# Whole-chunk 32-row products, grouped transposes, and no 32-row unit for the first expert

## The chip, the cores and the metric

One core of a Trainium2 chip runs the whole kernel. The metric is the device time of one execution in microseconds (us). The engines that matter here are TensorE (PE in the profile: matrix products; PEld is its loading of the stationary operand), VectorE (DVE), ScalarE (ACT), GpSimd (POOL, which issues gathers and scatters) and SyncE (SP, which issues the loads of weights).

## What is computed

A layer with token mixers and then a mixture of experts over 1024 tokens. The change lies in the expert stage and in the routing just ahead of it. Cut to that part, the reference is:

```
logits = h @ w_router + b_router
probs = softmax(logits).reshape(n_tok, 4, 4)
g_sel = argmax(top_k(probs, 2)[0].sum(-1), -1)
top_w, top_i = top_k(probs[token, g_sel], 2)
weight = top_w / sum(top_w)
expert = g_sel * 4 + top_i
...
y_blk = (silu(xb @ w_g[e]) * (xb @ w_u[e])) @ w_d[e]
...
y = sum(y_blk[dest] * weight, 1)
x = x + gt2 * y
return rms_norm(x, g_final)
```

There are 16 experts; each takes 1024 features to 1536 and back. Every token goes to two of them, 2048 slots in all. Everything is float32. With the inputs of the reference the sixteen experts receive 124, 123, 98, 103, 151, 157, 145, 139, 99, 152, 152, 85, 172, 80, 138 and 130 rows (worked out from the reference).

## The kernel before

**Pages.** An expert's weights come in 18 pages of 1 MB, each 128 x 2048: twelve for gate and up (`w_gu`), six for down (`w_d`). `load` takes the next page from `order` and issues it on SyncE into one of ten page buffers (tiles `praw` and `raw`); a buffer is free again when its last reader is done. `part` splits a page for products of full accuracy out of the faster float32r format: ScalarE rounds the page to its high part, VectorE subtracts to get the low part, and both stand in a tile `hl` with three buffers (lines 1186 and 1187). `page` hands out the next split page.

**Rows of an expert.** The rows of an expert are laid out as a block of 128 (block A) and 0, 1 or 2 units of 32 rows more (block B). `UNITS` fixes the number for each place in the order of the experts: the first place is always the model's expert 0, the others are sorted by their number of rows at run time. Before, the first place has one unit, the second two, eight others one, and six none. Rows beyond 128 plus 32 for each unit go to a slow loop at the end of the kernel (`overflow_block`), which is skipped when there are none.

**Block A** (`block_a`, line 1366). Per page there are two slices of 128 features, and for each slice the three products high x high, high x low and low x high, each over two halves of 512 columns: twelve matmuls, accumulated in `pa`.

**Block B** (`block_b`, line 1378). The 32 rows of a unit are multiplied with the unsplit page in plain float32. The array is used as four column strips of 32: strip g holds the unit's rows and computes the columns 256 g to 256 g + 255. That is eight matmuls for a page and a unit; the trace has two records for each. With two units a product of zeros (`pb<-zz`, line 1372) opens the accumulation.

**The loop over experts.** Gate and up come in three chunks of four pages, then the six down pages. Before, the products go in pairs of pages: block B of two pages, block A of the same two pages, and so on. So a chunk has two blocks B and the down part three. After a chunk, ScalarE applies silu to the gate half and VectorE multiplies by the up half: `sa` from `pa`, `sb_` from `pb`. TensorE then turns them (transposes `aat`, `abt`, lines 1573 and 1578), and they are copied out: `aah` and `aal` by `split_a`, `abT` by ScalarE. They are the stationary operand of the down products. During the down pages `prep` turns the next expert's gathered rows (`xat`, `xbt`), and at the end the sums are scaled (`ya`, `yb`) and added to rows of `x1_d` by indirect DMAs of GpSimd (line 1422).

**The first expert.** `own_row` and `own_rows` find its rows before the table of all experts is ready: per block of 128 tokens a mark matrix `own` (line 1131), then small products (line 1139) and a few steps on VectorE that give `tk0` and `ch0`, whose values drive the first gathers (`first_xa`, `first_xb`). After its first chunk, `places` works out on VectorE the order of all other experts and their rows (lines 1311 to 1342); SyncE reads three words of it (`cnt`) before it can address the pages of the second expert.

**The order of instructions.** Each engine runs its own queue in order. A list scheduler orders the instructions; `tc.issue_after(x)` puts the instructions traced in its block behind x on x's engine. In the last expert (no unit), `tail` starts the final normalisation of the rows that are already complete.

Of the kernel before, what the change touches and what calls it, by code (L numbers as in the profile page):

```python
# [6 lines left out]
F32 = mybir.dt.float32  # L7
F32R = mybir.dt.float32r
BF16 = mybir.dt.bfloat16
# [44 lines left out]
UNITS = tuple(2 if r == 1 else 1 if r < 10 else 0 for r in RANK)  # L54
# [24 lines left out]
def constants():  # L79
    p = np.arange(128)  # L80
    s, t = p[:, None], p[None, :]
    f = np.concatenate([
        np.eye(128),
        np.ones((128, 128)),
        (s < t) * 1.0,
        (s % 32) == np.arange(2),
    ], 1).astype(np.float32)
    t64 = np.arange(64)[None, :]
    i = np.concatenate([
        (s % 64) <= t64, (s % 64) >= t64,  # L90
        2 * (s + 128 * (np.arange(16) // 2)[None, :]) + (np.arange(16) % 2)[None, :],
        np.broadcast_to(2 * (S + np.arange(CAP) % TRASH)[:, None], (CAP, 16)).reshape(128, 144),
    ], 1).astype(np.int32)
# [12 lines left out]
    sl[:, 3] = 15 - e + 65536 * (e == 0)  # L106
    c = np.arange(128)[None, :]
    g4, r = s // 32, s % 32
    trash = np.concatenate([S + s, 4 * (S + 128 + r) + g4, 4 * (S + 160 + r) + g4], 1)
    z = np.concatenate([  # L110
        np.broadcast_to(16 * np.concatenate([c, 128 + c % 32, 160 + c % 32], 1), (128, 384)),
        np.broadcast_to([[32, 128, 128]], (128, 3)), np.broadcast_to([[1, 4, 4]], (128, 3)),
        np.concatenate([0 * s, g4, g4], 1) - trash, trash,
        np.stack([s // 32 + 4 * np.arange(8)[None], np.broadcast_to(s % 32, (128, 8)), np.ones((128, 8)),
                  np.zeros((128, 8))], 2).reshape(128, 32),
    ], 1).astype(np.float32)
    return f, i, g.reshape(128, 96), ((s - t) % 32 == 0).astype(np.float32), z, sl.reshape(128, 64)
# [48 lines left out]
def body(tc, A, out):  # L166
# [778 lines left out]
    tk0, ch0 = (cp.tile([128, 3], I32, name=n) for n in ("tk0", "ch0"))  # L945
# [27 lines left out]
    kz = t1.tile([128, 428], F32, name="kz")  # L973
# [11 lines left out]
    V.tensor_copy(tri.rearrange("p i c -> p (i c)"), kz[:, 396:428])  # L985
# [142 lines left out]
    def own_row(i):  # L1128

        R = st_[i][5]  # L1130
        V.tensor_scalar(own[:, i, :], kz[:, 0:384], R[:, 7, 0:1], R[:, 5, 0:1], op0=ALU.is_equal, op1=ALU.mult)
        V.tensor_copy(tri[:, i, 3:4], R[:, 4, 0:1])

    def own_rows():

        p = ax("own")
        for b in range(3):
            for i in range(8):
                PE.matmul(p[:, 4 * b:4 * b + 4], own[:, i, 128 * b:128 * b + 128], tri[:, i, :], start=i == 0,
                          stop=i == 7)  # L1140
        f = t1.tile([128, 3, 4], F32, name="f3")
        V.tensor_copy(f.rearrange("p b c -> p (b c)"), p[:, 0:12])
        for c in range(3):
            V.tensor_mul(f[:, :, c], f[:, :, c], kz[:, 384 + 3 * c:387 + 3 * c])
        V.tensor_add(f[:, :, 0], f[:, :, 0], f[:, :, 1])
        V.tensor_add(f[:, :, 2], f[:, :, 2], kz[:, 393:396])
        V.tensor_add(f[:, :, 0], f[:, :, 0], f[:, :, 2])
        placed.append(V.tensor_copy(tk0, f[:, :, 0]))
        V.tensor_copy(ch0, f[:, :, 3])
# [10 lines left out]
    raws, ready = [], []  # L1160
# [17 lines left out]
    def load():  # L1178
        raws.append(page_tile([128, 2048]))
        e, n, i = order.pop(0)  # L1180
        return SP.dma_start(raws[-1], A[n][bass.ds(expert(e), 1), i].rearrange("o p n -> (o p) n") if e else A[n][0, i])

    def part():
        raw = raws.pop(0)
        hl = split_tile()
        SC.activation(hl[:, 0, :], raw, AF.Copy)  # L1186
        V.tensor_sub(hl[:, 1, :], raw, hl[:, 0, :].bitcast(F32))  # L1187
        ready.append(tuple(a.rearrange("p (k n) -> p k n", k=2) for a in (raw, hl[:, 0, :], hl[:, 1, :])))

    def page():  # L1190
        if not ready:
            if not raws:
                load()
            part()
        return ready.pop(0)
# [84 lines left out]
    with tc.issue_after(counted.ins), tc.issue_after(scaled.ins):  # L1280
        for i in range(2):
            part()
# [77 lines left out]
    def block_a(acc, st, k0, pg, start, stop):  # L1360

        _, wh, wl = pg
        for k in range(2):
            for n, (x, w) in enumerate(((0, wh), (0, wl), (1, wh))):
                for h in range(2):
                    PE.matmul(acc[h], st[x][:, k0 + k, :], w[:, k, 512 * h:512 * h + 512],  # L1366
                              start=start and (k, n) == (0, 0), stop=stop and (k, n) == (1, 2))

    def block_b(n, acc, st, k0, pgs, first, last):

        if n > 1 and first:
            PE.matmul(acc, zz[:, 0:128], zz, start=True, stop=False)
        for i, (w, _, _) in enumerate(pgs):
            for j in range(n):
                for k in range(2):
                    end = last and (i, j, k) == (len(pgs) - 1, n - 1, 1)
                    for g in range(4):
                        PE.matmul(acc[32 * g:32 * g + 32, 256 * j:256 * j + 256], st(j, k0 + 2 * i + k),
                                  w[:, k, 256 * g:256 * g + 256], start=n == 1 and first and (i, k) == (0, 0), stop=end,
                                  tile_position=(0, 32 * g))  # L1380
# [165 lines left out]
    wAB = prep_a(0, *first_xa, ch0[:, 0:1]), prep_b(0, first_xb[0], lambda j: ch0[:, j + 1:j + 2])  # L1546
    before = []
    for e in range(E):
        U = UNITS[e]
        for c in range(3):  # L1550
            pa, pb = [pt(f"pa{h}", "pa", 4) for h in range(2)], pt("pb", "pb", 2) if U else None
            for i in range(0, 4, 2):
                pgs = [page() for k in range(2)]
                first = e + c + i == 0
                if not first:
                    block_b(U, pb, xb_, 2 * i, pgs, i == 0, i == 2)
                for k in range(2):
                    block_a(pa, XA, 2 * (i + k), pgs[k], i + k == 0, i + k == 3)
                if first:
                    block_b(U, pb, xb_, 2 * i, pgs, i == 0, i == 2)  # L1560
            if U:
                sb_ = ep_.tile([128, 2, 128], F32, name="sb_", bufs=2)
                pv = pb.rearrange("p (j u n) -> p j u n", j=2, u=2)[:, 0:U]
                SC.activation(sb_[:, 0:U], pv[:, :, 0], AF.Silu)
                V.tensor_mul(sb_[:, 0:U], sb_[:, 0:U], pv[:, :, 1])
            p = pt("aat", "pt", 2)
            for h in range(2):
                sa = ep_.tile([128, 2, 128], F32, name="sa", bufs=4)
                pv = pa[h].rearrange("p (g u n) -> p g u n", g=2, u=2)
                SC.activation(sa, pv[:, :, 0], AF.Silu)  # L1570
                mul = V.tensor_mul(sa, sa, pv[:, :, 1])
                for k in range(2):
                    PE.transpose(p[:, 256 * h + 128 * k:256 * h + 128 * k + 128], sa[:, k, :], ident)
            split_a(p, aah[:, 4 * c:4 * c + 4, :], aal[:, 4 * c:4 * c + 4, :])
            if U:
                p = pt("abt", "pt", 2)
                for j in range(U):
                    PE.transpose(p[:, 128 * j:128 * j + 128], sb_[:, j, :], ident)
                SC.activation(abT[:, c, 0:U].rearrange("p j t -> p (j t)"), p[:, 0:128 * U], AF.Copy)
            if c == 0:  # L1580
# [10 lines left out]
        for i in range(0, 6, 2):  # L1591
            pgs = [page() for k in range(2)]
            block_b(U, pb, ab_, 2 * i, pgs, i == 0, i == 4)
            for k in range(2):
# [3 lines left out]
            if e + 1 == E:  # L1598
                tail(f"d{i}")
# [66 lines left out]
```

## Time and profile before

| | us |
|---|---|
| median of three runs | 2281.84 |
| lowest and highest run | 2281.76, 2284.72 |
| the profiled execution | 2284.32 |
| its span, first to last instruction | 2282.5 |
| first matmul of the first expert, from the span's start | 1183.51 |
| last matmul of the last expert ends about | 2264.5 |

TensorE's mean granted clock over the span is 0.985. The expert stage takes about 1081 of the 2282.5 us. A timeline row has the start, the duration of the group (with its overlap in the pipeline: the distance between starts tells what it costs), engine, line, operation, operands, and the number of records; in brackets stand an idle time ahead of it and what ended that. A row of the waits has the waiting instruction, what it waited for, then us in total, times, and the longest one.

### The profile page before, as it was taken

The page shows a single profiled execution, that of the slowest core. Times are in us where ns is not written, and L with a number is a line of the kernel's source. Part 1 is how long each engine was busy: PE and PEld are TensorE (multiplying, and loading weights), DVE is VectorE, ACT ScalarE, POOL GpSimd, SP SyncE. Part 2 cuts the span into 40 slices and gives each one's busy share as a digit, 9 for nine tenths or more (in the row PEclk, how much of TensorE's full clock was granted, in tenths as well). Part 3 has the DMA queues.
Part 4 walks back from the last instruction along what each step waited for, and adds up shares of the span by engine and source line. Part 5 has one row for each costly group of instructions (what it writes and reads, how often), then busy time and mean ns, then how long its engine had stood idle before and what let it go on. Part 6 is the DMA issues. An engine that isn't in the chain of part 4 may idle for free. (4 is left out here: it accounts for less than half of the span.)

```text
span 2282.5 us, 36688 instructions
## 1 busy us (share of the span) xinstructions
PE 2207.9 (97%) x14595; PEld 1785.5 (78%) x14596; DVE 1417.8 (62%) x2135; ACT 1059.9 (46%) x1334; POOL 205.0 (9%) x176
## 2 busy tenths in 40 slices
PE   9999999999999999999969999999999999999975
PEld 6999898888889978888957677777777777777654
DVE  5644215846762354246877568786868687666667
ACT  3312125534542153233235456665757565555554
POOL 0011000000000000001331110000101010100031
PEclk9999999999999999999979999999999999999988
DMA  7665433656741366445658679797979798877774
GB/s 291 195 207 170 154 128 105 195 179 194 233 169 59 116 220 225 157 129 204 186 194 304 228 279 347 285 362 289 366 283 375 288 348 303 288 278 278 261 254 161
DMA packets 141986, 530.06 MB, mean 232 GB/s; under 512 B 17159, under 2 KB 57919, under 8 KB 94705
## 3 DMA queue, kind: packets, MB, share of 16 engines
q1 hardware_dynamic: 119584, 467.97, 56.2%
q0 software_dynamic: 21072, 55.43, 8.8%
q10 hardware_dynamic: 1152, 4.26, 0.5%
q8 instruction: 116, 1.90, 0.3%
q14 instruction: 62, 0.50, 0.1%
HBM read 457.36 MB, written 70.44 MB: 231 GB/s over the span
## 5 line engine op out<-in xcount | busy, mean ns | idle before, releaser
L1187 DVE TENSOR_TENSOR hl<-praw,hl 128x2048 fp32r<-128x2048 f32 x174 | 402.0, 2313 | 157.6 <-ACT hl L1186 155.1
L1366 PE MATMUL pa<-hl,xah 128*128 128x512 f32 x1536 | 437.1, 403 | 16.1 <-ACT hl L1186 11.4
L1186 ACT ACTIVATE hl<-praw 128x2048 fp32r<-128x2048 f32 x174 | 333.1, 1915 | 206.2 <-PE pa L1366 206.1
L1366 PEld LDWEIGHTS pa<-hl,xah 128*128 128x128 f32 x1536 | 284.7, 189 | 98.4 <-issue 17.3
L1187 DVE TENSOR_TENSOR hl<-raw,hl 128x2048 fp32r<-128x2048 f32 x114 | 261.0, 2291 | 114.4 <-ACT hl L1186 113.0
L1186 ACT ACTIVATE hl<-raw 128x2048 fp32r<-128x2048 f32 x114 | 218.4, 1916 | 139.2 <-PE pa L1366 135.1
L1366 PE MATMUL pa<-hl,xal 128*128 128x512 f32 x768 | 243.1, 397 | 0.0
L1366 PE MATMUL pa<-hl,aah 128*128 128x512 f32 x768 | 219.3, 403 | 5.7 <-DVE hl L1187 4.5
L256 PE MATMUL mm<-wh,hxh 128*128 128x256 f32 (+1 forms) x768 | 218.3, 284 | 4.6 <-DVE vv L285 3.5
L256 PE MATMUL mm<-wl,hxh 128*128 128x256 f32 (+1 forms) x768 | 216.6, 282 | 0.0
L256 PE MATMUL mm<-wh,hxl 128*128 128x256 f32 (+1 forms) x768 | 215.8, 281 | 0.0
L256 PE MATMUL mm<-hxh,wh 128*128 128x512 f32 x448 | 178.7, 399 | 0.0
L256 PE MATMUL mm<-hxh,wl 128*128 128x512 f32 x448 | 178.6, 399 | 0.0
L256 PE MATMUL mm<-hxl,wh 128*128 128x512 f32 x448 | 178.4, 398 | 0.0
L1366 PEld LDWEIGHTS pa<-hl,aah 128*128 128x128 f32 x768 | 141.8, 189 | 45.5 <-DVE hl L1187 5.4
L1366 PEld LDWEIGHTS pa<-hl,xal 128*128 128x128 f32 x768 | 144.1, 189 | 34.3
L256 PEld LDWEIGHTS mm<-wh,hxh 128*128 128x128 f32 x768 | 145.2, 189 | 5.6 <-DVE vv L285 3.8
L256 PEld LDWEIGHTS mm<-wl,hxh 128*128 128x128 f32 x768 | 145.3, 189 | 0.0
L256 PEld LDWEIGHTS mm<-wh,hxl 128*128 128x128 f32 x768 | 145.0, 189 | 0.0
L238 DVE TENSOR_TENSOR wl<-wraw,wh 128x2048 fp32r<-128x2048 f32 (+1 forms) x36 | 82.7, 2298 | 100.1 <-ACT wh L237 78.8
L1366 PE MATMUL pa<-hl,aal 128*128 128x512 f32 x384 | 121.6, 398 | 0.0
L237 ACT ACTIVATE wh<-wraw 128x2048 fp32r<-128x2048 f32 (+1 forms) x36 | 69.1, 1918 | 69.9 <-PE mm L256 67.7
(503 smaller groups left out, 3623.4 us busy)
## 6 DMA issues: line engine op xcount, KB each, us to landing
praw<-in_w_gu_dram SPq DMA_DIRECT2D x116, 1024.0 KB, 6.8
raw<-in_w_gu_dram SPq DMA_DIRECT2D x76, 1024.0 KB, 7.2
praw<-in_w_d_dram SPq DMA_DIRECT2D x58, 1024.0 KB, 8.1
raw<-in_w_d_dram SPq DMA_DIRECT2D x38, 1024.0 KB, 7.5
wraw<-in_w_in_dram SPq DMA_DIRECT2D x24, 1024.0 KB, 4.8
wraw<-in_w_mod_dram SPq DMA_DIRECT2D x18, 1024.0 KB, 5.7
vb<-v_d POOLq DMA_DIRECT2D x16, 1024.0 KB, 6.8
xt<-in_x_dram SPq DMA_DIRECT2D x16, 512.0 KB, 5.7
```

The costliest lines, as they stand in the source:

```text
L237: SC.activation(wh[:, :n], raw[:, :n], AF.Copy)
L238: V.tensor_sub(wl[:, :n], raw[:, :n], wh[:, :n].bitcast(F32))
L256: end = PE.matmul(acc, Wst[a](k), Wmv[b](k), start=n == 0, stop=n == tot - 1)
L1186: SC.activation(hl[:, 0, :], raw, AF.Copy)
L1187: V.tensor_sub(hl[:, 1, :], raw, hl[:, 0, :].bitcast(F32))
L1366: PE.matmul(acc[h], st[x][:, k0 + k, :], w[:, k, 512 * h:512 * h + 512], start=start and (k, n) == (0, 0), stop=stop and (k, n) == (1, 2))
```

## The change

Five things change.

1. The first expert has no 32-row unit any more. What found the unit's rows goes (`own` has 128 columns instead of 384, `own_rows` makes 8 products instead of 24), and so does its gather.
2. Block B runs over all four pages of a chunk at once, ahead of block A of these pages, and over three down pages at once. For this `raw_pages` hands out pages that are loaded and not yet split; `part` splits a given page when block A needs it.
3. The turning of a chunk (`turned_a`) is no longer done at its end. It stands behind the next chunk's block B, or, without a unit, behind block A of the next chunk's first page, and the four transposes of `sa` are one group.
4. The next expert's rows are turned ahead of the fourth down page, before it was after the fourth.
5. Tables that held the numbers of the first expert's unit shrink.

```
-UNITS = tuple(2 if r == 1 else 1 if r < 10 else 0 for r in RANK)
+UNITS = tuple(0 if r == 0 else 2 if r == 1 else 1 if r < 10 else 0 for r in RANK)
...
-    own = t1.tile([128, 8, 384], BF16, name="own")
+    own = t1.tile([128, 8, 128], BF16, name="own")
...
-        V.tensor_scalar(own[:, i, :], kz[:, 0:384], R[:, 7, 0:1], R[:, 5, 0:1], op0=ALU.is_equal, op1=ALU.mult)
+        V.tensor_scalar(own[:, i, :], kz[:, 0:128], R[:, 7, 0:1], R[:, 5, 0:1], op0=ALU.is_equal, op1=ALU.mult)
...
+    def raw_pages(n):
+
+        while len(pages) < n:
+            load()
+        return [p[0].rearrange("p (k n) -> p k n", k=2) for p in pages[:n]]
+
+    def part(i):
+
+        raw, hl = pages[i]
+        if hl is None:
+            hl = split_tile()
+            SC.activation(hl[:, 0, :], raw, AF.Copy)
+            V.tensor_sub(hl[:, 1, :], raw, hl[:, 0, :].bitcast(F32))
+            pages[i][1] = hl
+        return hl
...
-    first_xb = gather_b(0, lambda j: tk0[:, j + 1:j + 2])
-    with tc.issue_after(first_xb[1][-1].ins):
+    with tc.issue_after(first_xa[1].ins):
         scatter(7)
...
+    def turned_a(c, sas, sb_, U, behind):
+
+        with tc.issue_after(behind.ins):
             p = pt("aat", "pt", 2)
+            for k in range(4):
+                PE.transpose(p[:, 128 * k:128 * k + 128], sas[k // 2][:, k % 2, :], ident)
             split_a(p, aah[:, 4 * c:4 * c + 4, :], aal[:, 4 * c:4 * c + 4, :])
             if U:
                 p = pt("abt", "pt", 2)
                 for j in range(U):
                     PE.transpose(p[:, 128 * j:128 * j + 128], sb_[:, j, :], ident)
                 SC.activation(abT[:, c, 0:U].rearrange("p j t -> p (j t)"), p[:, 0:128 * U], AF.Copy)
...
-            for i in range(0, 4, 2):
-                pgs = [page() for k in range(2)]
-                first = e + c + i == 0
-                if not first:
-                    block_b(U, pb, xb_, 2 * i, pgs, i == 0, i == 2)
-                for k in range(2):
-                    block_a(pa, XA, 2 * (i + k), pgs[k], i + k == 0, i + k == 3)
...
+            if U:
+                end = block_b(U, pb, xb_, 0, raw_pages(4), True, True)
+                if left:
+                    turned_a(*left, end)
+            for k in range(4):
+                end = block_a(pa, XA, 2 * k, page(), k == 0, k == 3)
+                if k == 0 and left and not U:
+                    turned_a(*left, end)
...
-        for i in range(0, 6, 2):
-            pgs = [page() for k in range(2)]
-            block_b(U, pb, ab_, 2 * i, pgs, i == 0, i == 4)
-            for k in range(2):
-                block_a(pa, AA, 2 * (i + k), pgs[k], i + k == 0, i + k == 5)
-            if i == 2 and e + 1 < E:
+        for i in range(0, 6, 3):
+            if U:
+                end = block_b(U, pb, ab_, 2 * i, raw_pages(3), i == 0, i == 3)
+                if i == 0:
+                    turned_a(*left, end)
+            if i == 3 and e + 1 < E:
                 wAB = prep(e + 1, *nxt)
+            for k in range(i, i + 3):
+                end = block_a(pa, AA, 2 * k, page(), k == 0, k == 5)
+                if k == 0 and not U:
+                    turned_a(*left, end)
```

On TensorE, this is the end of the first chunk of the fourth expert (one unit) before; `x16` are the eight matmuls of block B for each of two pages:

```order
L1366 MATMUL pa_13137<-hl,xal 128x512
L1378 MATMUL pb<-praw,xbT 32x256 x16
L1573 MATMUL aat<-kf,sa 128x128 x2
L1578 MATMUL abt<-kf,sb__13239 128x128
L1366 MATMUL pa_13264<-hl,xah 128x512
L1573 MATMUL aat<-kf,sa 128x128 x2
L1366 MATMUL pa_13265<-hl,xah 128x512
```

And the same place in the changed kernel:

```order
L1367 MATMUL pa_12942<-hl,xal 128x512
L1380 MATMUL pb<-praw,xbT 32x256 x32
L1557 MATMUL aat<-kf,sa 128x128 x4
L1562 MATMUL abt<-kf,sb__13044 128x128
L1367 MATMUL pa_13059<-hl,xah 128x512
```

The block has doubled, all transposes stand behind it in one group, and no further block comes before the chunk ends.

On VectorE, this is a part of the place computation in the first expert before, with the splits of pages (`hl`) between its steps:

```order
L1187 TENSOR_TENSOR hl<-praw,hl 128x2048
L1325 TENSOR_TENSOR w_11565<-sel,fi 128x256
L1326 TENSOR_REDUCE fo<-w_11565 128x16
L1187 TENSOR_TENSOR hl<-praw,hl 128x2048
L1328 TENSOR_TENSOR key<-fo,ks 1x16
```

In the changed kernel:

```order
L1189 TENSOR_TENSOR hl<-praw,hl 128x2048
L1326 TENSOR_TENSOR w_11492<-sel,fi 128x256
L1422 TENSOR_TENSOR aal<-aat,aah 128x512
L1327 TENSOR_REDUCE fo<-w_11492 128x16
L1189 TENSOR_TENSOR hl<-praw,hl 128x2048
L1329 TENSOR_TENSOR key<-fo,ks 1x16
```

The steps stand between the splits as before; what moved is `aal`, which was ahead of these rows.

On SyncE, these are the loads issued around the first expert's start before:

```order
L1181 DMA praw<-in_w_gu_dram 128x2048 x4
L1017 DMA x_d<-x_11042 128x1024
L1295 DMA quarter<-in_kg_dram 128x1
L1297 DMA ks<-in_ks_dram 128x64
L1354 DMA g2A<-mod_d 128x1024
L1357 DMA g2B<-mod_d 32x256 x4
L210 DMA gf<-in_rows_dram 128x1024
L1291 DMA ids<-tab 128x16
```

And in the changed kernel:

```order
L1175 DMA praw<-in_w_gu_dram 128x2048 x4
L1013 DMA x_d<-x_11042 128x1024
L1175 DMA praw<-in_w_gu_dram 128x2048
L1296 DMA quarter<-in_kg_dram 128x1
L1298 DMA ks<-in_ks_dram 128x64
L1355 DMA g2A<-mod_d 128x1024
L1292 DMA ids<-tab 128x16
```

The eleventh page is now ahead of the small loads, and `gf` has left for a place among the second expert's pages.

More of the change, by code (lines that the diff above doesn't have):

```diff
@@ L1136, in own_rows @@
         p = ax("own")
[L1137 to L1149, printed above, removed]
+        for i in range(8):
+            PE.matmul(p[:, 0:4], own[:, i, :], tri[:, i, :], start=i == 0, stop=i == 7)
+        f = t1.tile([128, 4], F32, name="f3")
+        V.tensor_mul(f[:, 0:3], p[:, 0:3], kz[:, 128:131])
+        V.tensor_copy(f[:, 3:4], p[:, 3:4])
+        V.tensor_add(f[:, 0:1], f[:, 0:1], f[:, 1:2])
+        V.tensor_add(f[:, 2:3], f[:, 2:3], kz[:, 131:132])
+        V.tensor_add(f[:, 0:1], f[:, 0:1], f[:, 2:3])
+        placed.append(V.tensor_copy(tk0, f[:, 0:1]))
+        V.tensor_copy(ch0, f[:, 3:4])
     def scatter(i):
@@ L1178, in load @@
     def load():
-        raws.append(page_tile([128, 2048]))
         e, n, i = order.pop(0)
[L1181 to L1188, printed above, removed]
-    def page():
[L1191 to L1195, printed above, removed]
+        raw = page_tile([128, 2048])
+        pages.append([raw, None])
+        return SP.dma_start(raw, A[n][bass.ds(expert(e), 1), i].rearrange("o p n -> (o p) n") if e else A[n][0, i])
+    def raw_pages(n):
[10 more added lines that the diff above has]
+        return hl
+    def page():
+        raw_pages(1)
+        hl = part(0)
+        pages.pop(0)
+        return tuple(hl[:, j, :].rearrange("p (k n) -> p k n", k=2) for j in range(2))
     for i in range(8):
@@ L1365, in block_a @@
                 for h in range(2):
-                    PE.matmul(acc[h], st[x][:, k0 + k, :], w[:, k, 512 * h:512 * h + 512],
-                              start=start and (k, n) == (0, 0), stop=stop and (k, n) == (1, 2))
+                    end = PE.matmul(acc[h], st[x][:, k0 + k, :], w[:, k, 512 * h:512 * h + 512],
+                                    start=start and (k, n) == (0, 0), stop=stop and (k, n) == (1, 2))
+        return end
     def block_b(n, acc, st, k0, pgs, first, last):
@@ L1372, in block_b @@
             PE.matmul(acc, zz[:, 0:128], zz, start=True, stop=False)
-        for i, (w, _, _) in enumerate(pgs):
+        for i, w in enumerate(pgs):
             for j in range(n):
                 for k in range(2):
-                    end = last and (i, j, k) == (len(pgs) - 1, n - 1, 1)
+                    stop = last and (i, j, k) == (len(pgs) - 1, n - 1, 1)
                     for g in range(4):
-                        PE.matmul(acc[32 * g:32 * g + 32, 256 * j:256 * j + 256], st(j, k0 + 2 * i + k),
-                                  w[:, k, 256 * g:256 * g + 256], start=n == 1 and first and (i, k) == (0, 0), stop=end,
-                                  tile_position=(0, 32 * g))
+                        end = PE.matmul(acc[32 * g:32 * g + 32, 256 * j:256 * j + 256], st(j, k0 + 2 * i + k),
+                                        w[:, k, 256 * g:256 * g + 256], start=n == 1 and first and (i, k) == (0, 0),
+                                        stop=stop, tile_position=(0, 32 * g))
+        return end
     def weight(x, ch, name):
@@ L1579, in body @@
                 SC.activation(abT[:, c, 0:U].rearrange("p j t -> p (j t)"), p[:, 0:128 * U], AF.Copy)
+    for e in range(E):
+        U = UNITS[e]
+        left = None
+        for c in range(3):
+            pa, pb = [pt(f"pa{h}", "pa", 4) for h in range(2)], pt("pb", "pb", 2) if U else None
+            if U:
[7 more added lines that the diff above has]
+            if U:
+                sb_ = ep_.tile([128, 2, 128], F32, name="sb_", bufs=2)
+                pv = pb.rearrange("p (j u n) -> p j u n", j=2, u=2)[:, 0:U]
+                SC.activation(sb_[:, 0:U], pv[:, :, 0], AF.Silu)
+                V.tensor_mul(sb_[:, 0:U], sb_[:, 0:U], pv[:, :, 1])
+            sas = []
+            for h in range(2):
+                sa = ep_.tile([128, 2, 128], F32, name="sa", bufs=4)
+                pv = pa[h].rearrange("p (g u n) -> p g u n", g=2, u=2)
+                SC.activation(sa, pv[:, :, 0], AF.Silu)
+                mul = V.tensor_mul(sa, sa, pv[:, :, 1])
+                sas.append(sa)
+            left = c, sas, sb_ if U else None, U
             if c == 0:
```

43 lines of the change are left out of this document (11 added, 32 removed).

## The prediction

> **What bounds the kernel now.** I read the page's busy shares first, then the waits of the expert stage (1380 us to the end, twelve of its sixteen experts and the tail), then TensorE's timeline of single experts.
>
> ```profile
> span 2282.5 us, 36688 instructions
> PE 2207.9 (97%) x14595; PEld 1785.5 (78%) x14596; DVE 1417.8 (62%) x2135; ACT 1059.9 (46%) x1334; POOL 205.0 (9%) x176
> ```
> ```profile
> ACT hl L1186 <- PE pa L1366: 271.7, 179, 5.5
> DVE hl L1187 <- ACT hl L1186: 204.4, 168, 2.5
> PE pa L1366 <- ACT hl L1186: 12.5, 2, 11.4
> PE pa L1366 <- DVE hl L1187: 9.1, 6, 3.9
> ```
>
> The columns of the waits are us in total, times, and the longest. TensorE is busy 97% of the span. The two engines that split weight pages wait for it (ScalarE 271.7 us for a free `hl` buffer), while it waits 21.6 us for them, nearly all in the last expert. So time is saved only where TensorE itself has less to do, as long as the splits keep up. The scatter of each expert's result marks the experts' lengths:
>
> ```profile
> 1259.27 3.37 POOL L1422 DMA_INDIRECT x_d<-ya,tks  x1 [4.39 <-DVE ya L1612]
> 1349.67 3.18 POOL L1422 DMA_INDIRECT x_d<-ya,tks  x1 [3.89 <-DVE ya L1612]
> 1401.96 3.36 POOL L1422 DMA_INDIRECT x_d<-ya,tks  x1 [36.01 <-DVE ya L1612]
> 1473.69 3.37 POOL L1422 DMA_INDIRECT x_d<-ya,tks  x1 [3.74 <-DVE ya L1612]
> ```
>
> An expert with two 32-row units takes 90.4 us (1349.67 - 1259.27), one with none 52.3, one with one unit 71.7.
>
> **Part 1: no unit for the first expert.** Its TensorE work runs from the first row below to the first product of the second expert, the second row:
>
> ```profile
> 1183.51 1.22 PE L1366 MATMUL pa<-hl,xah 128*128 128x512 f32 x2
> 1255.99 0.39 PE L1372 MATMUL pb<-zz 128*128 128x512 f32 x1
> ```
>
> That is 72.5 us, 0.7 more than the later one-unit experts. Without the unit I expect 52.3 + 0.7 = 53.0 if nothing else comes late. But something does: VectorE's place computation sits in this expert alone, between these rows.
>
> ```profile
> 1201.56 0.15 DVE L1384 COPY wA<-xa 128x1 f32<-128x1 f32 x1
> 1219.26 0.13 DVE L1342 CAST cnt<-rank 1x1 int32<-1x1 f32 x1
> 1201.56:1219.33 17.77, 17.77 (x128) 12.64 (x127) 17.29 (x50) 9.82 (x11) 0.44 (x1) 1.00 0.84 292
> L1187 DVE TENSOR_TENSOR hl<-praw,hl 128x2048 fp32r<-128x2048 f32 x174 | 402.0, 2313 | 157.6 <-ACT hl L1186 155.1
> L1186 ACT ACTIVATE hl<-praw 128x2048 fp32r<-128x2048 f32 x174 | 333.1, 1915 | 206.2 <-PE pa L1366 206.1
> ```
>
> In those 17.8 us VectorE is busy 17.3; four page splits (2.3 each, fourth row) take 9.2 of it, and two products `sa`, one `aal` and one `sb` about 1.7 more, so the places cost about 6.4 us. TensorE did not feel it, because the unit's 32-row products stretched the pages. Now it takes a page each 2.8 us (twelve matmuls of 0.232, from the spacing quoted in part 2). Count from the first matmul: page 5 is split at 12.6 us (its buffer is free at 8.4, ScalarE takes 1.9, VectorE 2.3). Until page 11, VectorE then does six splits (six at 2.2 from start to start, 13.2), two pairs of `sa` (1.5), two `aal` (1.4) and the places (6.2 without the unit's weight): 12.6 + 22.3 = 34.9. TensorE wants that page's low part at 11 x 2.8 + 0.4 for transposes + 0.5 for its first two matmuls = 31.7. The difference, 3.2 to 3.8 us with the splits at their whole 2.3, is new waiting; I take 3.5. The first expert then takes 56.5: **-16.0 us**. Ends: no waiting (-19.5) and all 6.4 us of the places (-13.1).
>
> The path before it also changes. The product that marks rows shrinks from 384 to 128 columns; the last of them stands on the chain to the first gather, and that gather is what TensorE waits for:
>
> ```profile
> 1172.78 0.48 DVE L1131 TENSOR_SCALAR own<-kz,R 128x384 bf16<-128x384 f32 x1
> 1181.71 1.97 PE L1395 MATMUL xat<-kf,xa 128*128 128x128 f32 x8 [7.78 <-DMA xa<-h_d,tk]
> 1360.00:1380.00 20.00, 20.00 (x91) 16.12 (x90) 17.82 (x13) 14.94 (x11) 2.31 (x1) 1.00 1.01 421
> ```
>
> It can win at most about 0.5 there. Against it, SyncE's queue now issues the eleventh page as soon as page 0 is split, ahead of the small loads, and that 1 MB moves beside the gather; at the 421 GB/s of the last row it is 2.5 us at most. Half a MB (`gf`) leaves the same place. I take 0, ends -0.5 and +2.5. The rows moved behind that page (`ks`, `quarter`, `g2A`) are wanted some 12 us after the first matmul or later.
>
> **Part 2: 32-row products at once.** Each of the nine experts that keep a unit had nine such blocks and now has five: three pairs over the up and gate chunks become one block each, three over the down pages become two. What a block costs beyond its products:
>
> ```profile
> 1406.18 0.63 PE L1366 MATMUL pa<-hl,xal 128*128 128x512 f32 x2
> 1406.74 1.93 PE L1378 MATMUL pb<-praw,xbT 128*32 128x256 f32 x32
> 1408.61 1.19 PE L1366 MATMUL pa<-hl,xah 128*128 128x512 f32 x4
> 1409.64 0.63 PE L1366 MATMUL pa<-hl,xal 128*128 128x512 f32 x2
> 1410.11 1.09 PE L1366 MATMUL pa<-hl,xah 128*128 128x512 f32 x4
> 1411.04 0.63 PE L1366 MATMUL pa<-hl,xal 128*128 128x512 f32 x2
> ...
> 1286.03 3.66 PE L1378 MATMUL pb<-raw,xbT 128*32 128x256 f32 x64
> 1289.62 1.20 PE L1366 MATMUL pa<-hl,xah 128*128 128x512 f32 x4
> ```
>
> From start to start, four matmuls take 0.93 in the stream (1410.11 to 1411.04) and 1.03 just after a block; two take 0.47 in the stream and 0.56 just before one. A block of 32 records (16 matmuls in two passes) lasts 1.87, one of 64 lasts 3.59, so two of 32 hold 0.15 more. One block fewer saves 0.10 + 0.09 + 0.15 = 0.34 us. Four fewer in nine experts: 36 x 0.34 = **-12.2 us**.
>
> **Part 3: the transposes move.** They go behind the next block (or behind the next chunk's first page), four together.
>
> ```profile
> 1414.38 1.93 PE L1378 MATMUL pb<-praw,xbT 128*32 128x256 f32 x32
> ...
> 1418.34 1.10 PE L1366 MATMUL pa<-hl,xah 128*128 128x512 f32 x4
> ...
> 1297.51 0.66 PE L1573 MATMUL aat<-kf,sa 128*128 128x128 f32 x4
> 1298.00 0.38 PE L1578 MATMUL abt<-kf,sb__12350 128*128 128x128 f32 x2
> 1298.32 1.93 PE L1378 MATMUL pb<-praw,xbT 128*32 128x256 f32 x32
> ...
> 1392.24 1.03 PE L1395 MATMUL xat<-kf,xa 128*128 128x128 f32 x8
> 1393.03 1.18 PE L1366 MATMUL pa<-hl,aah 128*128 128x512 f32 x4
> ```
>
> The first stretch is a one-unit chunk end of before: 3.96 us, less the block (1.87), six matmuls (1.40) and the 0.10 behind the block, leaves 0.59 for five transposes mixed among matmuls. Six in a row took 0.81 (the next three rows), eight 0.79 (the last two). So five in a row cost 0.50 to 0.68; I take 0.68, the row that also stands behind a block: +0.09 in 24 chunks, **+2.2 us**. In the seven experts without a unit, four in a row cost about 0.4 + 0.1 of switching, against about 0.44 mixed in: 21 chunks, **+1.0**. TensorE hardly waited for `sa` before, so hiding that wait wins nothing. Ends of both together: -2.2 and +6.
>
> In the last expert some of the vector work of the final normalisation changes places with splits, by one 1.3 us product each way: 0, ends -2.5 and +2.5.
>
> **Sum.** -16.0 - 12.2 + 2.2 + 1.0 = -25.0. The profiled execution took 2284.32 us around its span of 2282.5, the median of the runs is 2281.84; its span becomes 2257.5 and the median **2257**.
>
> **Rivals.** *The first expert does not stall.* The unit's 19.5 us all go; the sum is -28.5, 2253. For it: the next page's two first matmuls need only ScalarE's half. Against it: the count of VectorE's work above.
>
> *The first expert stalls longer, and the clock falls.*
>
> ```profile
> 2230.83 0.74 PE L1366 MATMUL pa<-hl,xah 128*128 128x512 f32 x2 [2.59 <-DVE hl L1187]
> 2248.94 1.22 PE L1366 MATMUL pa<-hl,aah 128*128 128x512 f32 x2 [3.93 <-DVE hl L1187]
> ```
>
> Two matmuls took 0.74 after an idle of 2.59 us and 1.22 after 3.93. My waits fall in several pieces, none above 2. In one piece of 6.4 they would add about 2.5 for slow matmuls: 3 + 2.5 more, plus 2.5 from a late gather, gives -17, 2265. The Trainium skill ("TensorE: Matmul & The Clock Gate", part 1) states that an idle window of about 3.4 us halves the clock for another such window; both rows agree with it, and by it the forecast stands unless the waits fuse.
>
> *The merged blocks starve the splits* (slower). Four full pages now run without a 32-row block between. The fourth page's buffer comes free 2.8 us after the block, is split 4.2 later (1.9 + 2.3) and its low part is wanted at 8.4 + 0.5: 1.9 of slack. If ScalarE and VectorE put more than that between, each of 45 blocks loses the rest; from 0.55 us a block the gain is gone, at 1 us (45 - 25) the kernel is 20 us slower, 2302. Against it: experts without a unit run eighteen pages like that and take 52.3 us for 18 x 2.79 = 50.2 plus transposes. In the new order the `sb` activation waits for the block in front of later splits on ScalarE, but at that time all three buffers are full.
>
> *The first expert overflows.* Its room falls from 160 rows to 128, and rows beyond that go through a separate loop of 18 pages, 45 us at 421 GB/s and a second normalisation. The reference's inputs send 124 rows to it, so this needs five more.
>
> **How the numbers follow.** Forecast 0.63 (2253 to 2262), no stall 0.13, longer stall 0.15, starving 0.08 (half of it ending within 0.2%, half slower), overflow 0.01. A measurement of this kernel can tell about 0.2%, 4.6 us. Faster 0.91, same 0.04, slower 0.05. The range, 2248 to 2266, takes in the ends of the stall, of the transposes and of the start, and leaves out the starving.
>
> **What would show it.** The first expert's matmuls in 55 to 58 us, with waits for VectorE's `hl` of 3 to 4 us there; one-unit experts of 70.6 instead of 71.7; experts without a unit still 52.3 to 52.5; about 45 blocks. Wrong would be waits of TensorE for `hl` in the middle experts, a gap at raw pages before a block, or a first matmul after 1185.

## The result, and the profile after

| | median us | runs | against before (95% interval) |
|---|---|---|---|
| before | 2283.28 | 2281.76 to 2292.34 | |
| after | **2254.43** | 2249.74 to 2258.37 | 0.9865 (0.985 to 0.988) |
| predicted | 2257 | 2248 to 2266 | |

The kernel is 1.35% faster. The medians differ by 28.9 us, and the interval stands for 27 to 34 us; my sum was 25.0. The median lies within the stated range, but the gain was larger than the sum. The terms below are read from one execution of each kernel. That of after took 2258.37 us, the longest of its four runs, and its span is 25.9 us shorter than that of before (2282.5 - 2256.6). The total came out close. Its terms did not, and two of them were wrong for reasons that I had not seen.

The page of after, span and busy shares:

```profile
span 2256.6 us, 36047 instructions
PE 2175.3 (96%) x14286; PEld 1785.9 (79%) x14287; DVE 1414.2 (63%) x2127; ACT 1056.8 (47%) x1327; POOL 213.3 (9%) x174
```

Its waits from 1380 us to the end (us in total, times, longest):

```profile
ACT hl L1188 <- PE pa L1367: 215.1, 187, 5.1
DVE hl L1189 <- ACT hl L1188: 187.3, 172, 3.5
PE pa L1367 <- ACT hl L1188: 14.5, 2, 13.1
PE pa L1367 <- DVE hl L1189: 9.5, 4, 5.0
```

TensorE still sets the pace: ScalarE waits for it 215.1 us, less than the 271.7 of before, and TensorE waits for split pages 24.0 us, nearly all in the last expert as before. The merged blocks do not starve the splits. The scatters that mark the experts' lengths:

```profile
1249.06 3.43 POOL L1425 DMA_INDIRECT x_d<-ya,tks  x1 [15.13 <-DVE ya L1627]
1335.17 3.36 POOL L1425 DMA_INDIRECT x_d<-ya,tks  x1 [8.15 <-DVE ya L1627]
1388.10 3.18 POOL L1425 DMA_INDIRECT x_d<-ya,tks  x1 [36.89 <-DVE ya L1627]
1457.68 3.37 POOL L1425 DMA_INDIRECT x_d<-ya,tks  x1 [7.47 <-DVE ya L1627]
```

Two units take 86.1 us now (90.4 before), none 52.9 (52.3), one 69.6 (71.7; I had expected 70.6). From these I make three numbers for each kernel, which the experiments use:

- **first expert**: from its first matmul to its scatter, 65.1 us (before: 1259.27 - 1183.51 = 75.8). That is 10.6 less, where I had 16.0.
- **fourteen experts**: from the first expert's scatter to that of the fifteenth expert, 909.3 us (before 926.6). That is 17.3 less, where I had about 9 (12.2 less 2.2 and less 0.7, the share of the five experts without a unit that lie here).
- **tail**: from there to the end, 98.2 us (before 96.7), 1.6 more.

They are used because they repeat: the same kernel profiled again gave 64.7, 909.4 and 98.4, although its span was 5.5 us shorter, 5.2 of it ahead of the first expert's first matmul.

What happened in the first expert is in TensorE's timeline (start, duration, and in brackets the idle time before and what ended it):

```profile
1182.11 1.97 PE L1398 MATMUL xat<-kf,xa 128*128 128x128 f32 x8 [9.85 <-DMA xa<-h_d,tk]
1183.92 2.07 PE L1367 MATMUL pa<-hl,xah 128*128 128x512 f32 x4
...
1213.51 0.73 PE L1367 MATMUL pa<-hl,xah 128*128 128x512 f32 x2 [0.35 <-DVE hl L1189]
...
1220.60 0.73 PE L1367 MATMUL pa<-hl,xah 128*128 128x512 f32 x2 [0.76 <-DVE cnt L1343]
...
1234.53 1.27 PE L1398 MATMUL xat<-kf,xa 128*128 128x128 f32 x8 [2.92 <-DMA xa<-h_d,tks]
1235.45 2.05 PE L1367 MATMUL pa<-hl,aah 128*128 128x512 f32 x4
1237.30 1.05 PE L1367 MATMUL pa<-hl,aal 128*128 128x512 f32 x2
1238.16 1.32 PE L1367 MATMUL pa<-hl,aah 128*128 128x512 f32 x4
```

The waits for VectorE that I had put at 3.5 us are 1.1 (third and fourth row). In their place stands one that I had not thought of, 2.92 us for the gather of the second expert's rows, and behind it four matmuls take 1.85 us from start to start (1235.45 to 1237.30) where they take 0.93 in the stream. TensorE's granted clock reads 0.50 from 1235.4 to 1238.6, and 1.00 just before and after. The gather itself, on GpSimd, and VectorE at that time:

```profile
1218.52 7.34 POOL L1269 DMA_INDIRECT xa<-h_d,tks  x1 [37.36 <-DVE rank L1342]
1226.16 4.75 POOL L1269 DMA_INDIRECT xb<-h_d,tks  x1 [0.30 <-issue]
```
```profile
1218.27 2.27 DVE L1189 TENSOR_TENSOR hl<-praw,hl 128x2048 fp32r<-128x2048 f32 x1
1220.47 0.13 DVE L1343 CAST cnt<-rank 1x1 int32<-1x1 f32 x1
1220.53 4.47 DVE L1189 TENSOR_TENSOR hl<-raw,hl 128x2048 fp32r<-128x2048 f32 x2
1224.93 0.73 DVE L1588 TENSOR_TENSOR sa<-sa,pa 128x256 f32<-128x256 f32 x2
1225.60 4.48 DVE L1189 TENSOR_TENSOR hl<-raw,hl 128x2048 fp32r<-128x2048 f32 x2
1230.00 0.67 DVE L1422 TENSOR_TENSOR aal<-aat,aah 128x512 fp32r<-128x512 f32 x1
```

The same gather took 0.97 us in before:

```profile
1218.89 0.97 POOL L1267 DMA_INDIRECT xa<-h_d,tks  x1 [34.47 <-PE abt L1578]
```

Here it lasts from 1218.52 to 1225.86, which is 0.86 us past the end of three splits in a row (1225.00); the next gather ends at 1230.91, 0.83 past the end of the next two (1230.08). So the reading to be tested: while VectorE runs splits, which read two operands from SBUF, GpSimd cannot finish issuing an indirect DMA.

### The profile page after: what moved, and what is told of

Read it like the earlier page. It is cut to its first block, busy times and chain, and to the rows that moved or that the text cites. A ratio compares the mean times of both kernels' runs of the same rounds, so it can differ in the third digit from the quotient of the medians.

```text
span 2256.6 us, 36047 instructions
## 1 busy us (share of the span) xinstructions
PE 2175.3 (96%) x14286; PEld 1785.9 (79%) x14287; DVE 1414.2 (63%) x2127; ACT 1056.8 (47%) x1327; POOL 213.3 (9%) x174
## 3 DMA queue, kind: packets, MB, share of 16 engines
q8 instruction: 114, 1.87, 0.3%
## 5 line engine op out<-in xcount | busy, mean ns | idle before, releaser
L1367 PE MATMUL pa<-hl,xah 128*128 128x512 f32 x1536 | 429.4, 400 | 18.8 <-ACT hl L1188 13.1
L252 PE MATMUL mm<-wh,hxl 128*128 128x256 f32 (+1 forms) x768 | 215.1, 280 | 0.0
```

Source lines behind the costliest of these rows:

```text
L252: end = PE.matmul(acc, Wst[a](k), Wmv[b](k), start=n == 0, stop=n == tot - 1)
L1367: end = PE.matmul(acc[h], st[x][:, k0 + k, :], w[:, k, 512 * h:512 * h + 512], start=start and (k, n) == (0, 0), stop=stop and (k, n) == ( ...
```

## Experiments

Four questions: what each part is worth alone; what a block costs; why the gather is late; why the first matmuls are slow. Each kernel computes the whole result. All ratios are to the kernel before. Where an expectation names the length of the first expert, it counts to the second expert's first block (61.9 us in after), and not to the scatter (65.1).

### The parts, one at a time

**part1_only** is the kernel before with the new `UNITS`, `own_rows`, `kz` and first gather, and the old loop.

```
-    wAB = prep_a(0, *first_xa, ch0[:, 0:1]), prep_b(0, first_xb[0], lambda j: ch0[:, j + 1:j + 2])
+    wAB = prep_a(0, *first_xa, ch0), []
```

> The kernel before with part 1 alone: no unit for the first expert, rows and gathers as in the change, but 32-row blocks in pairs of pages and transposes at the chunk's end. Prediction's sum: -16.0 us against before, ratio 0.993, first expert 56.5 us with 3.5 us of waits for VectorE's hl. Rival from the trace of after (a late gather of the second expert's rows): that gather is wanted one page (2.8 us) later here, so its 2.9 us wait all but goes and the slow matmuls behind it too: first expert about 58, -14 us, ratio 0.994, hl waits of 1 us at most. If the first expert takes 61 to 62 us as in after, neither holds.

Measured: 2269.07 us, 0.9951 (0.9937 to 0.9965), 13.3 us less. First expert 64.5 (61.8 to the second expert's first block), fourteen experts 926.3 (unchanged), tail 96.6. Neither expectation holds: the first expert is as long as in after, with a wait of 2.57 us for the gather, 1.1 us of waits for `hl`, and slow matmuls:

```profile
1227.89 0.30 PE L1387 MATMUL xat<-kf,xa 128*128 128x128 f32 x1 [2.57 <-DMA xa<-h_d,tks]
...
1229.35 1.91 PE L1358 MATMUL pa<-hl,aah 128*128 128x512 f32 x4
```

The gather's instruction is held for less time than in after, 2.88 us beside one split. But one of the eight transposes of the second expert's rows stands 6.8 us ahead of the others in TensorE's order (1227.89 and 1234.69), so it meets the late gather too.

**unit_kept** is the change with the old `UNITS` and rows; in the first chunk the merged block stands behind the second page.

```
+            first = e + c == 0
...
+                if first and k == 1:
+                    block_b(U, pb, xb_, 0, w4, True, True)
```

> The change without part 1: the first expert keeps its 32-row unit, merged blocks and moved transposes everywhere. Prediction's terms: -12.2 +2.2 +1.0 = -9.0 us against before (ratio 0.996), with first expert near 71.7. Reading of the trace of after (experts 2 to 15 shorter by 17.3, tail 1.6 longer): about -17 us, ratio 0.9925, one-unit experts 69.7 us.

Measured: 2264.84 us, 0.9927 (0.9914 to 0.9941), 17.5 us less: the reading of the trace, not my terms. One-unit experts take 69.9 us. The split differs from that reading, though: the fourteen experts take 910.7, and the tail only 97.0.

**pairs** is the change with the blocks in pairs of pages again.

```
-                end = block_b(U, pb, xb_, 0, raw_pages(4), True, True)
+                if U and k % 2 == 0:
+                    end = block_b(U, pb, xb_, 2 * k, raw_pages(2), k == 0, k == 2)
```

> The change with its 32-row blocks in pairs of pages again (36 blocks more), transposes still behind the next block. Prediction's 0.34 us a block: +12.2 us against the change, one-unit experts 71.0. Rival, merging is worth more than I counted (17.3 + 3.2 = 20.5 us over 36 blocks, 0.57 each): +20 us, one-unit experts 71.9. Rival, the transposes and not the merging carry the extra gain: +12, and moving the transposes back costs 5.

Measured: 2269.12 us, 0.9946 (0.9933 to 0.996); the fourteen experts take 925.4, so 36 blocks more cost 16.0, or 0.44 each, between the two expectations (14.7 by the medians of the whole runs). Without the merging, the moved transposes, together with the earlier turning of the next expert's rows, are worth next to nothing: 925.4 against the 926.3 of part1_only.

**turn_at_end** is the change with merged blocks and the old transposes at the chunk's end.

```
+                for k in range(2):
+                    PE.transpose(p[:, 256 * h + 128 * k:256 * h + 128 * k + 128], sa[:, k, :], ident)
...
-                if left:
-                    turned_a(*left, end)
```

> The change with the transposes mixed into the chunk's end as before (part 3 undone), blocks merged. Prediction's +3.2 for part 3: 3.2 us faster than the change. Rival, transposes behind a block are cheaper than mixed (0.53 instead of 0.59, and one exit from short products instead of two): one-unit experts 70.1 to 70.6 instead of 69.7, experts without a unit 52.4 instead of 52.8, together 2 to 5 us slower than the change. A tail shorter by 1.6 would say that the moved vector work made it longer.

Measured: 2280.93 us, 0.9994 (0.9985 to 1.0003). Neither expectation comes near: nearly the whole gain of the change is gone. The fourteen experts take 938.4, which is 29.1 more than in after and 12.1 more than with the old blocks. These are from the longest of its twelve runs (2290.83 us), but the ratios of the whole runs, against 0.9865 and 0.9883 for the change, say 25 to 29 us too. The tail is 98.3 as in after, so the moved transposes are not what makes it longer. The chunk end in TensorE's timeline:

```profile
1405.06 1.93 PE L1380 MATMUL pb<-praw,xbT 128*32 128x256 f32 x32
1406.98 0.44 PE L1572 MATMUL aat<-kf,sa 128*128 128x128 f32 x2
1407.26 0.27 PE L1577 MATMUL abt<-kf,sb__13044 128*128 128x128 f32 x1
1407.46 0.62 PE L1380 MATMUL pb<-praw,xbT 128*32 128x256 f32 x2
1408.01 0.44 PE L1572 MATMUL aat<-kf,sa 128*128 128x128 f32 x2
1408.38 1.93 PE L1380 MATMUL pb<-praw,xbT 128*32 128x256 f32 x30
1410.23 1.20 PE L1367 MATMUL pa<-hl,xah 128*128 128x512 f32 x4
```

and the same place in after:

```profile
1399.71 3.66 PE L1380 MATMUL pb<-praw,xbT 128*32 128x256 f32 x64
1403.30 0.66 PE L1557 MATMUL aat<-kf,sa 128*128 128x128 f32 x4
1403.80 0.27 PE L1562 MATMUL abt<-kf,sb__13044 128*128 128x128 f32 x1
1403.83 1.18 PE L1367 MATMUL pa<-hl,xah 128*128 128x512 f32 x4
```

The transposes stand about 1.9 us behind the chunk's last product, where `sa` is expected. In before a block of two pages (1.87 us) is just over by then. A block of four pages is only half done: the transposes break it into three pieces, and the stretch takes 5.17 us (1405.06 to 1410.23) instead of 4.12 (1399.71 to 1403.83). That is 1.05 in each of 27 chunks with a unit, 28.4 of the 29.1.

### What a block costs

**single** is the change with a block for every page, and the transposes behind the second.

```
+                if U:
+                    end = block_b(U, pb, xb_, 2 * k, raw_pages(1), k == 0, k == 3)
+                    if left and k == 1:
+                        turned_a(*left, end)
```

> The change with a 32-row block for every page (18 in an expert instead of 5, 117 more in nine experts), the transposes behind the second block. If a block costs a fixed price for switching: 0.34 us each (my prediction's) gives +40 us against the change, one-unit experts 74.2; 0.41 (the run with pairs of pages: 14.7 us over 36) gives +48, one-unit experts 75.1. If the price is not one of the number of blocks but of what stands behind them: less than +20.

Measured: 2295.31 us, 1.0053 (1.0037 to 1.0068); the fourteen experts take 949.4, 40.0 more for 117 blocks: 0.342 us each. That is the price of the prediction. It is an average: one-unit experts that follow each other take 75.15 us instead of 70.24 (0.38 a block); where they alternate with experts without a unit, the two together take 126.9 instead of 122.5 (0.34 a block). In this kernel the transposes stand in one piece, as in after; in pairs they fall in two pieces among matmuls, as in before, which goes with the 0.1 more a block there. No run separates these two.

### Why the gather of the second expert is late

**after_again** is the change unaltered, for the same chip as the next three.

> The change once more, unaltered, to stand beside the next three on one chip. Every theory: ratio to before 0.9865 to 0.9875 (about -29 to -31 us); gather of the second expert's rows held on GpSimd for about 7 us and TensorE waiting about 2.9 us for it.

Measured: 2253.52 us, 0.9883 (0.9867 to 0.9899); gather 7.33 us, wait 2.82, first expert 64.7 (61.4 to the second expert's first block). The ratio is a little above the expected ones, which its interval takes in for the most part.

**hold_split**: three splits of the first expert wait for a small memset that stands behind the gather on GpSimd.

```
+            if 12 <= used[1] < 15:
+                tc.add_manual_dep(low.ins, marks[0].ins.name, SYNC, reason="behind the second gather")
...
+            with tc.issue_after(rows_a[1].ins):
+                marks.append(GP.memset(mark, 0.0))
```

> The change, but the split of page 11 and the next two of the first expert wait on VectorE until GpSimd has issued the second expert's gather. Theory (VectorE's splits, run one behind the other, keep GpSimd from writing the gather's descriptors): the gather's instruction takes 1 us instead of 7.3, its rows land 6 us earlier, TensorE's 2.9 us wait for them goes and so do some 2 us of slow matmuls; the split starts about 1.2 us later, which may show as up to 1.2 us more wait for hl: -3 to -5 us. Rival (the gather is slow because of the 0.4 MB that it moves beside the weight pages, whatever VectorE does): the instruction stays at 5 us or more, no gain.

GpSimd, then VectorE:

```profile
1216.26 0.97 POOL L1271 DMA_INDIRECT xa<-h_d,tks  x1 [37.11 <-DVE cnt L1345]
1217.23 0.12 POOL L1420 MEMSET mark<- 128x1 f32 x1
1217.53 2.98 POOL L1271 DMA_INDIRECT xb<-h_d,tks  x1 [0.18 <-issue]
```
```profile
1217.38 2.29 DVE L1189 TENSOR_TENSOR hl<-praw,hl 128x2048 fp32r<-128x2048 f32 x1 [1.12 <-DMA praw<-in_w_gu_dram]
```

With VectorE held back for 1.12 us (the row names a DMA, but ScalarE had read that page by 1211.94, so it had landed; the wait that I added is the one for GpSimd) the gather takes 0.97 us. The rows land 6.4 us after the issue instead of 15.8, and TensorE does not wait for them. The next gather, which meets the split again, takes 2.98. So VectorE's splits hold up the gather. The rival is out: the DMA engines were as busy during this gather as during the long one of after_again (95% and 96%). The time: 2251.88 us, 0.9866 (0.985 to 0.9882); first expert 61.7, 2.9 less than in after_again and so at the lower end of the 3 to 5 expected, while the wait for `hl` grew from 0.74 to 2.13. On the median of the runs that is 1.6, inside the intervals.

**early_rows** takes the row numbers of the 128-row gathers out of `places` as soon as their sum is there.

```
+            if i == 0:
+                V.tensor_copy(ids[:, 0], o[:, 0])
+                V.tensor_scalar(tkA, ids[:, 0], 1, None, op0=ALU.logical_shift_right)
+                V.tensor_scalar(chA, ids[:, 0], 1, None, op0=ALU.bitwise_and)
```

> The change, with the row numbers of the 128-row gathers taken out of the places as soon as their own sum is there, two sums ahead of the last. Theory (the gather is issued too late for a first expert that has become shorter): issued about 8 us earlier, near 1210 on the span of after; its rows land before they are wanted even if splits hold it for some us; the 2.9 us wait and 2 us of slow matmuls go: -5 us, first expert 57 instead of 61.9. Rival (VectorE's chain of places sets the first expert's length): waits for hl of VectorE grow instead, gain under 2 us.

```profile
1208.56 0.97 POOL L1269 DMA_INDIRECT xa<-h_d,tks  x1 [29.55 <-DVE w L1326]
1214.29 7.30 POOL L1269 DMA_INDIRECT xb<-h_d,tks  x1 [4.76 <-issue]
```

Measured: 2251.14 us, 0.9861 (0.9846 to 0.9876); first expert 61.5, 3.2 less than in after_again (58.3 to the second expert's first block, where 57 was expected), and no wait for the rows. The gather is early and short; now that of the unit's rows is held for 7.30, but nobody wants those so soon. Waits for `hl` are 0.91 (VectorE) and 1.58 (ScalarE), so part of the gain went to what the rival names.

**late_turn_first** puts the second expert's transposes two pages later.

```
+                if e == 0 and k == 4:
+                    wAB = prep(1, *nxt)
```

> The change, with the second expert's transposes behind the first expert's fifth down page instead of ahead of the fourth, two pages (5.6 us) later. Theory of the late gather: the wait of 2.9 us and the 2 us of slow matmuls behind it go, -5 us, first expert 57. Rival: the wait only moves, because the split of the transposed rows (xah, xal) is then too late for the second expert's first matmul; gain under 2 us and a wait for xah or xal at the start of the second expert.

Measured: 2249.99 us, 0.9854 (0.9841 to 0.9868); first expert 60.6, 4.0 less, with a wait of 0.38 for `xal` at the second expert's start, whose length grows by 0.7; over both that is 3.3. Here the gather still takes 7.34 us: it only has to be there in time.

### Why the first matmuls are slow

**early_mixed** is early_rows, with the transposes of experts without a unit at the chunk's end.

> The change with the early row numbers, and with the transposes of the experts without a unit mixed into the chunk's end as before (those of the others stay behind the merged block). Theory: experts without a unit go back from 52.73 to 52.45 us, seven of them -2 us; with the -3 us of the early rows the whole is 4 to 6 us faster than the change, ratio to before about 0.986. Rival, in the first expert the mixed transposes shift VectorE's work as in the run with part 1 alone, and a transpose of the second expert's rows moves up: nothing won beside the early rows.

Measured: 2252.63 us, 0.9861 (0.9843 to 0.9878). Experts without a unit take 52.8 as in after: the 0.25 us that they lost does not lie in their transposes. Nothing is won beside the early rows, as the rival says, but its reason is not seen: the eight transposes of the second expert's rows stand together (1229.52), and the first expert is 0.5 us shorter than in early_rows.

**warm_start** is early_mixed with 30 products in the wait for the first gather.

```
+    for _ in range(30):
+        PE.matmul(warm, hl0[:, 0, 0:128], hl0[:, 0, 0:512], start=True, stop=True)
```

> The kernel with early rows and mixed transposes, and 30 products of a split page with itself, whose result nobody reads, in the 9.8 us in which TensorE waits for the first gather. Theory (the first transposes and matmuls are slow because TensorE's clock fell during that idle time): eight xat transposes 0.8 to 1.0 us instead of 1.97, the first four matmuls 0.93 to 1.1 instead of 2.07, first expert with its start 2 to 3 us shorter. Rival (slow for another reason, such as loading of instructions or the first read of the page): no change. Should the 30 products outlast the wait, up to 1 us is lost.

```profile
1170.05 9.49 PE L1556 MATMUL warm<-hl 128*128 128x512 f32 x30
1180.14 1.09 PE L1402 MATMUL xat<-kf,xa 128*128 128x128 f32 x8 [0.59 <-DMA xa<-h_d,tk]
1180.98 0.48 PE L1378 MATMUL pb<-zz 128*128 128x512 f32 x1
1181.48 1.19 PE L1371 MATMUL pa<-hl,xah 128*128 128x512 f32 x4
```

Measured: 2249.75 us, 0.9845 (0.9826 to 0.9863). The eight transposes take 1.09 us instead of 1.97, the first four matmuls 1.19 instead of 2.07, and the first expert 59.6 after 61.0 in early_mixed. Three stretches of after and two of warm_start show the clock. A row has the stretch and its length, TensorE's busy time and its records, the granted clock, the share of the DMA engines, and GB/s:

```profile
1160.50:1164.00 3.50, 2.29 (x22) 0.50 0.64 218
1164.00:1170.00 6.00, 0.26 (x4) 0.50 0.11 42
1182.00:1186.00 4.00, 3.89 (x13) 0.50 0.17 47
```
```profile
1175.50:1180.00 4.50, 4.04 (x18) 1.00 1.01 397
1180.10:1183.00 2.90, 2.85 (x16) 1.00 0.12 33
```

In after the clock is at 0.50 some 12 us before the wait for the gather begins (1172.3), stays there through 6 us with 0.26 us of work, and is still there in the first matmuls. In warm_start it is back at 1.00 while the 30 products run, and stays there. So the slowness is that of the granted clock, and work given to TensorE ahead of the gather takes it away; but the clock had fallen before this wait, and not in it as the theory says. This kernel has the lowest median that I measured, hardly below late_turn_first (2249.99) and 4 us below the change (2253.52). Its interval lies below the one that the change had in after_again, and overlaps that of its first measurement (0.985 to 0.988) and that of early_mixed; the 1.4 us of the first expert stand against the 0.5 between the two profiles of the change.

## Why the prediction was right, and where it was not

**What bounds the kernel: right.** TensorE was the bound and stayed it. The middle experts have no waits for split pages, so "the merged blocks starve the splits" did not happen. Of the other rivals, "the first expert does not stall" was nearer than my 3.5 us for `hl` (1.1), and the fall of the clock came, but behind the wait for the gather.

**Part 1, the first expert: -10.6 instead of -16.0.** The step that failed is "But something does": I counted VectorE's work and looked for the wait at `hl`. VectorE was as full as counted, continuously busy from 1196.18 to 1230.67, and split the page that I had counted to (page 11) 36.6 us after the first matmul (1220.54), where I had 34.9. But TensorE wanted it only at 35.9, not at 31.7: slow matmuls at the start, products moved ahead and a wait had delayed it by then. So `hl` came only 1.1 us late in all instead of 3.5. The price was paid elsewhere: the full VectorE held GpSimd's gather for 7.34 us, and the shorter first expert, with the next expert's transposes a page earlier in its order, wanted those rows sooner. That cost 2.92 us, and 1.5 for slow matmuls behind it (twelve in 4.3 us, 1235.45 to 1239.79, for 2.8 at the stream's 0.233). With the gather in time and TensorE kept busy beforehand (warm_start) the first expert is 16.2 shorter than before. That this is close to my 16.0 does not confirm it, because warm_start also takes away slow matmuls that before has. Some 2 us of the 61.9 that after takes up to the second expert's first block I cannot place. From a row with 2.59 us of idle time and 0.74 for the two matmuls behind it I had taken that waits below 3 us hardly slow TensorE; here 2.92 was enough for a full slowing, and 2.57 in part1_only, where the clock reads 0.50 from 1228.6 to 1231.8. The length alone does not decide: after 2.64 us in the last expert of after the clock still reads 1.00 (2206.4 to 2210.0). The Trainium skill ("TensorE: Matmul & The Clock Gate", part 1) states an idle window of about 3.4 us; these two runs differ, with 2.92 and 2.57.

**The start: 0 right as far as can be told, but for the clock.** The first matmul came 0.4 us later than in before. That is one execution of each; in after_again, the same kernel, it came 5.2 us earlier, so a term of this size cannot be confirmed. Yet the first ten matmuls took 4.0 us (1183.92 to 1187.95 in after), and 3.0 in before, where two short transposes of 0.2 stand among them:

```profile
1184.53 0.45 PE L1406 MATMUL xbt<-kf,xb 128*128 128x128 f32 x2
...
1186.69 0.63 PE L1366 MATMUL pa<-hl,xal 128*128 128x512 f32 x2
```

The granted clock, 0.50 until then, comes back to 1.00 3.0 us after the first transpose `xat` in before (at 1184.7) and 5.3 us after it in after (at 1187.5). I had put no price on that. Nor does it belong to the change for certain: in after_again the ten matmuls took 3.6 us after an idle time of 9.71, about the same as the 9.85 in after.

**Part 2, a block's price of 0.34: right, and confirmed at 0.342.** But the step that called it -12.2 by itself was wrong. Without part 3, with the transposes left where they were, merging costs 12.1 us in the fourteen experts. The blocks are whole only because of part 3.

**Part 3, +3.2: wrong in sign and in kind.** I priced the transposes by how long five of them last (0.68, then 0.53 in after) and compared with before, where they stand behind a block of two pages by the luck of timing. What counted was where they would stand once the block was twice as long: in its middle. Given merged blocks, part 3 is worth 29.1 us; without them about 1. (The +1.0 for experts without a unit was also added up too low: 0.4 + 0.1 against 0.44 in 21 chunks is 1.3.) The row for it was there, in before, behind the block that starts at 1414.38 and is over after 1.87:

```profile
1416.33 0.44 PE L1573 MATMUL aat<-kf,sa 128*128 128x128 f32 x2
```

The order of a kernel with part 2 alone would have shown the rest.

**What the 17.3 consist of.** 36 blocks at 0.342 are 12.3. Another 3.7 is what pairs lost beyond that (16.0), where the transposes fall in two pieces, and 1.2 lies between before and pairs (926.6 to 925.4); I have not taken these two apart further, and that the 3.7 come from the two pieces is argued, not shown.

**The sum.** First expert -10.6, start +0.4, fourteen experts -17.3, tail +1.6: -25.9. Part 1 was 5.4 too hopeful, parts 2 and 3 together 8.3 too timid; that they nearly cancel is luck, and the reason why the total was close. What makes the tail 1.6 us longer stays open: it is 98.3 in turn_at_end and 96.5 in pairs, so it goes with the merged blocks there, but unit_kept has merged blocks too and shows 97.0.

## What to carry to other kernels

When two edits touch the same stretch of an engine's order, price them together: lay out where each instruction stands with one edit and without the other before adding their terms. When one engine gets fuller, look not only at who waits for its results but at what else its instructions hold up, and when a stage gets shorter, ask of every transfer that starts in it whether it still lands in time. A few products that nobody reads, placed in a known long wait of TensorE, can cost less than the slow matmuls after it; here that was worth 1.4 us.

## What the runs showed of the hardware

- **Splits on VectorE hold up an indirect DMA's issue.** A gather that meets no split at its start takes 0.95 to 1.00 us; beside one split 1.35 to 3.03, by how much of the split is left; beside three in a row 7.3, ending 0.8 to 0.9 us after the last. The Trainium skill ("SBUF — State Buffer", section "Who interferes with whom") states that a VectorE instruction with two SBUF inputs contends with a GpSimd instruction that reads SBUF, and that the lock on the ports which they share is exclusive; the trace agrees, for the indirect DMA takes its row numbers (`tks`) from SBUF. The same section of the Trainium skill infers that a `tensor_tensor` does not stall the generation of descriptors; the 7.3 us here differ from that. That GpSimd can be held through a whole run of such instructions is what these traces add. It is not always: scatters that meet two splits in a row (1335.17 in after) end 1.4 us after the first of them, and in after the first gather began at 1174.27 beside a split that ended at 1175.44 and was done at 1176.31, in the middle of the next split. Why it got in there and not at 1220.47 stays open.
- **An interruption of a block of 32-row products is dear.** Two interruptions by transposes cost 1.05 us, and each block that is entered and left 0.34.
- **A wait below 3 us can halve TensorE's clock, or leave it.** After 2.57 and 2.92 us without work it read 0.50 for about 3.4 us; after 2.59 and 2.64 it stayed at 1.00.
- **The stretch ahead of the expert stage varies most.** Its first matmul came between 1176.7 and 1186.2 us in thirteen profiles of kernels that differ little or not at all up to there, while the fourteen experts of one kernel repeated within 0.1 us in its two profiles. Effects of 3 us in one stage are read better from its own length than from the whole time.
